# Banded attention: scores of even and odd heads issued alternately into two PSUM banks, softmax by token tile, and one pool of eight PSUM banks

## The chip, the cores and the metric

The kernel runs on one core of one Trainium2 chip. The metric is device time in microseconds (us), from the start of the program to its end; the median of the runs counts. The core has a matrix engine (TensorE, PE in the profile, with its weight loads as PEld), a vector engine (VectorE, DVE), an activation engine (ScalarE, ACT), a general one (GpSimd, POOL), and a queue engine that issues DMAs (SyncE, SP). Matmul results land in PSUM, which has eight banks of 128 x 512 float32.

## The reference, cut to what matters

One sequence of 512 tokens with 1024 channels passes two blocks of two layers each: a gated recurrence with a convolution, cross-attention to a memory, feed-forward layers, a second gated recurrence, and then, near the end, the layer of this change, a causal sliding-window attention with 16 query heads of 64 channels, two key/value heads, a window of 128, a bias by distance and a sink logit for each head. Cut:

```
q = (h @ w_q)                                   # 16 heads of 64, in two groups of 8
s = q k^T / 8  over 128 queries x 256 keys      # the block before and the block itself
s = where(mask, s + bias, NEG)
m = max(max(s), sink);  p = exp(s - m)
p = p / (sum(p) + exp(sink - m))
out = (p @ v) @ w_out
```

After it come a last layer of 1024 to 4096 to 1024 channels and a norm.

## The kernel before, in words

Everything is float32. A product is made of three matmuls (`mm3`, lines 180 to 182): each operand is split into a high part (`split`, L152, ScalarE) and the rest (L153, VectorE), and high x high, high x low and low x high are added up in PSUM. Weights come by DMA into `raw`, are split into `w` tiles (`chunk`) and used by `lin_a` (output channels on partitions, four banks at once), `lin_b` (tokens on partitions) or `lin_out` (the last product of a layer, with residual and norm). The order of the instructions on each engine is not written by hand: a scheduler runs through the program with its own estimate of times, takes what is ready by the order in the text (moved by `later` and by `ahead`), and gives a tile its place in a pool when its first writer is issued. Each engine then runs its own list in that order, with semaphores between.

PSUM is divided into two pools. `mm` has five banks (`bank`), for the projections and for the accumulators of attention and recurrence; `aux` has three (`xbank`), for transposes, scores and other short-lived results. SBUF has a pool `big` of 16 slots of 8 KB a partition, from which most activations come, the score tiles `s` among them.

The banded attention is `swa` (L931). Keys are computed once and laid out twice, on partitions 0 to 63 and 64 to 127, as `K`; values lie in `vz`. For each of the two groups of 8 heads (j = 0, 1) `q_proj(j)` makes the queries `qh`, `ql`, in which an even head has partitions 0 to 63 and its odd neighbour 64 to 127, and `attend(j)` calls `swa_heads` (L995). That goes through eight units (t, e): four tiles of 128 tokens, and for each the even (e = 0) and the odd (e = 1) four heads. `soft` makes the scores of a unit: twice a bank with two heads, six matmuls of 64 rows by 256 keys; VectorE scales the bank and adds the bias into `s` (L1014); then maximum (L1017, L1018), exponentials on ScalarE (L1021), sums and sink (L1023 to L1026), and the division, half on VectorE (L1029), half on ScalarE (L1031). `apply` transposes `s` (L1043), splits it into `pT` (tiles of `ring`, one for each e), and multiplies by the values into `po`, one bank for a whole token tile, which is split into `oh`, `ol` after e = 1. `staged` (its fourth argument is 2 here) writes `soft` of two units ahead of each `apply`. `q_proj(1)` stands behind `attend(0)` in the text, and `attend(1)` lies inside `lin_out` of the output projection, behind its early part, which multiplies the first half of the heads into four banks that stay open.

Of the kernel before, what the change touches and what calls it, by code (L numbers as in the profile page):

```python
# [10 lines left out]
F32 = mybir.dt.float32  # L11
# [3 lines left out]
ALU = mybir.AluOpType  # L15
# [57 lines left out]
class Net:  # L73
    def __init__(self, tc, a, ctx):
        self.tc, self.nc, self.a = tc, tc.nc, a
        pool = lambda name, bufs, **kw: ctx.enter_context(tc.tile_pool(name=name, bufs=bufs, **kw))
        self.const = pool("const", 1)
        self.wp = pool("wp", 4)
        self.rawp = pool("rawp", 3)
        self.big = pool("big", 16)  # L80
        self.work = pool("work", 2)
        self.small = pool("small", 4)
        self.mm = pool("mm", 5, space=bass.MemoryType.PSUM)
        self.aux = pool("aux", 3, space=bass.MemoryType.PSUM)
        self.n = 0
        nc = self.nc
        self.consts = self.const.tile([128, NCONST], F32, name="consts")
        nc.sync.dma_start(self.consts[:, :DEC], a["consts"][:, :DEC])
        self.ident = self.consts[:, IDENT:IDENT + 128]
        self.steps = self.const.tile([128, 256], F32R, name="steps")  # L90
        nc.scalar.activation(self.steps, self.consts[:, TRI:TRI + 256], AF.Copy)
        self.gains_T = self.const.tile([128, 40], F32, name="gains_T")
        self.half = self.const.tile([128, 8], F32, name="half")
        nc.gpsimd.memset(self.half, -0.5)
        self.r = []
        for t in range(4):
            self.r.append(self.const.tile([128, 1024], F32, name=f"r{t}"))
            nc.sync.dma_start(self.r[t], a["x"][0, t * 128:(t + 1) * 128, :])
            if t == 1:
                self.first = self.chunk(a["ab_w_in"][0], 2560, ahead=0)  # L100
# [29 lines left out]
        return bank  # L130

    def xbank(self, shape):
        return self.aux.tile(shape, F32, tag="aux", name=self.nm("aux"))

    def bload(self, dst, ap):
        self.nc.sync.dma_start(dst, ap.unsqueeze(0).broadcast_to(list(dst.shape)))
# [156 lines left out]
        else:  # L293
            self.nc.vector.tensor_tensor(r, r, ps, ALU.add)  # L294

# [1 line left out]

    def hgrn_mixer(self):
        nc, a = self.nc, self.a
# [504 lines left out]
            first = False  # L804


# [1 line left out]

    def gla_prepare(self):
        nc, a = self.nc, self.a  # L810
# [184 lines left out]
    def swa_heads(self, j, qh, ql, K, vz, bias, sink, nsink, oh, ol):  # L995
        nc = self.nc
        po = self.ready(self.bank([128, 4, 128]))

        def keys(t):
            k0 = max(t - 1, 0) * 128  # L1000
            return (k0, 0, 256) if t else (k0, 128, 128)

        def soft(u):
            t, e = u
            tk = slice(t * 128, t * 128 + 128)
            k0, off, n = keys(t)
            rows = slice(64 * e, 64 * e + 64)
            s = self.slot([128, 4, 256], name="s")
            for i in range(0, 4, 2):
                ps = self.xbank([128, 2, 256])  # L1010
                for d in range(2):
                    self.mm3(ps[:, d, :], qh[rows, i + d, tk], ql[rows, i + d, tk],
                             K[rows, j, 0, k0:k0 + 256], K[rows, j, 1, k0:k0 + 256], True, True)
                nc.vector.scalar_tensor_tensor(s[:, i:i + 2, :n], ps[:, :, :n], 0.125,  # L1014
                                               bias[:, e, i:i + 2, off:off + n], ALU.mult, ALU.add)
            mx = self.st([128, 4], "mx4")
            nc.vector.reduce_max(mx, s[:, :, :n], axis=AX.X)  # L1017
            nc.vector.scalar_tensor_tensor(mx, mx, -1.0, nsink[:, j, e], ALU.mult, ALU.min)  # L1018
            sm = self.st([128, 4], "sm4")
            for h in range(4):  # L1020
                nc.scalar.activation(s[:, h, :n], s[:, h, :n], AF.Exp, bias=mx[:, h:h + 1],  # L1021
                                     accum_out=sm[:, h:h + 1])
            nc.vector.tensor_tensor(mx, mx, sink[:, j, e], ALU.add)  # L1023
            nc.scalar.activation(mx, mx, AF.Exp)
            nc.vector.tensor_tensor(sm, sm, mx, ALU.add)
            nc.vector.reciprocal(sm, sm)  # L1026
            for h in range(4):
                if h < 2:
                    nc.vector.tensor_scalar(s[:, h, :n], s[:, h, :n], sm[:, h:h + 1], None, ALU.mult)  # L1029
                else:  # L1030
                    nc.scalar.activation(s[:, h, :n], s[:, h, :n], AF.Identity, scale=sm[:, h:h + 1])  # L1031
            return s

        def apply(u, s):
            t, e = u
            tk = slice(t * 128, t * 128 + 128)
            k0, off, n = keys(t)
            nk = n // 128
            p = self.ring[e]
            for kt in range(nk):  # L1040
                ps = self.xbank([128, 4, 128])
                for i in range(4):
                    nc.tensor.transpose(ps[:, i, :], s[:, i, kt * 128:kt * 128 + 128], self.ident)  # L1043
                self.split(p[:, 0, kt], p[:, 1, kt], ps)
            c = slice(64, 192) if e == 0 else slice(0, 128)
            for kt in range(nk):
                kb = k0 // 128 + kt
                self.mm3(po, vz[0][:, kb, j, c], vz[1][:, kb, j, c], p[:, 0, kt], p[:, 1, kt],
                         kt == 0 and e == 0, kt == nk - 1 and e == 1)
            if e == 1:  # L1050
                self.split(oh[:, :, tk], ol[:, :, tk], po)

        self.staged([(t, e) for t in range(4) for e in range(2)], soft, apply, 2)


def body(tc, a, out, stop=None):
# [66 lines left out]
```

## Time and profile before

| | |
|---|---|
| time, median of 3 runs | 2504.81 us (2504.08 to 2505.48) |
| span of the profiled execution, first to last instruction | 2503.4 us |
| mean granted TensorE clock | 0.993 |
| busy share: PE, PEld, DVE, ACT, POOL | 98%, 82%, 50%, 38%, 7% |
| DMA, mean over the span | 96 GB/s |

Times of instructions are counted from the start of the span, which is 1.4 us shorter than the median. Matmuls are pipelined: a row's duration reaches from its start to the landing of its results, so that a matmul of 0.28 us can be followed by the next after 0.12 us; what TensorE can do in a time is read from the distance of starts. A row "x2" merges neighbours of the same kind. In brackets stands how long the engine had waited for nothing but another engine, and which.

### The profile page before, as it was taken

What the parts mean: (1) busy time and instruction counts of PE and PEld (TensorE: products, weight loads), DVE (VectorE), ACT (ScalarE), POOL (GpSimd) and SP (SyncE); (2) the same over time, 40 slices, a digit from 0 to 9 for tenths busy, and PEclk for the clock granted to TensorE, in tenths of its full rate; (3) what the DMA queues carried; (4) which work ended last, traced back from release to release, by engine and by line L of the source; (5) the groups of instructions that cost most, each with busy time, mean ns of one, the idle gap of its engine ahead of it and who ended that gap; (6) DMA issues with size and microseconds to landing.
All of it is one profiled execution on the core that took longest, in us unless ns stands there. A gap on an engine that the chain in (4) does not pass through costs nothing.

```text
span 2503.4 us, 30298 instructions
## 1 busy us (share of the span) xinstructions
PE 2458.3 (98%) x12334; PEld 2052.4 (82%) x12334; DVE 1249.7 (50%) x1772; ACT 944.6 (38%) x1576; POOL 181.3 (7%) x219
## 2 busy tenths in 40 slices
PE   8989999999999999999999999999999999999998
PEld 8876787888888997888888786888888877888887
DVE  4798566433326766433327423444444467444443
ACT  3643343222223343322224634433223456423323
POOL 1151300000000100000001003100000100000000
PEclk9999899999999999999999999999999999999999
DMA  6323122333324332233223223233222421222222
GB/s 214 109 102 102 53 85 77 92 99 95 99 74 144 123 130 76 85 101 99 95 76 121 69 85 43 76 101 101 93 101 98 142 74 51 72 97 95 99 93 84
DMA packets 121788, 239.48 MB, mean 96 GB/s; under 512 B 7849, under 2 KB 14309, under 8 KB 121392
## 3 DMA queue, kind: packets, MB, share of 16 engines
q1 hardware_dynamic: 118976, 229.73, 28.3%
q0 software_dynamic: 2096, 6.76, 1.4%
q8 instruction: 97, 1.59, 0.3%
q10 hardware_dynamic: 576, 1.05, 0.1%
q14 instruction: 43, 0.35, 0.0%
HBM read 234.34 MB, written 6.32 MB: 96 GB/s over the span
## 4 chain that ended last, share of the span: by engine, by line
PE 90%; DVE 6%; issue 1%; ACT 1%; DMA 1%; POOL 0%; SPq 0%; POOLq 0%; DVEq 0%; ACTq 0%
PE mm L180 28%; PE mm L181 27%; PE mm L182 27%; DVE acc L525 2%; PE aux L254 2%; PE aux L581 1%; DVE w L153 1%; PE aux L180 1%; PE mm L608 1%; PE mm L605 1%; PE aux L182 1%; PE aux L181 1%; DVE bn L275 0%; PE aux L1043 0%; DMA raw<-in_ffn_wg 0%
## 5 line engine op out<-in xcount | busy, mean ns | idle before, releaser
L153 DVE TENSOR_TENSOR w<-raw,w 128x1024 fp32r<-128x1024 f32 (+1 forms) x286 | 341.0, 1195 | 604.4 <-ACT w L152 604.1
L181 PE MATMUL mm<-xTl,w 128*128 128x512 f32 (+1 forms) x1696 | 614.0, 363 | 2.2 <-DVE xTl L153 2.2
L180 PE MATMUL mm<-xTh,w 128*128 128x512 f32 (+1 forms) x1696 | 610.4, 363 | 1.0 <-ACT w L152 0.8
L182 PE MATMUL mm<-xTh,w 128*128 128x512 f32 (+1 forms) x1696 | 605.7, 362 | 0.0
L152 ACT ACTIVATE w<-raw 128x1024 fp32r<-128x1024 f32 (+1 forms) x286 | 293.8, 1029 | 748.8 <-PE mm L182 598.3
L181 PEld LDWEIGHTS mm<-xTl,w 128*128 128x128 f32 x1696 | 321.5, 190 | 50.8 <-DVE xTl L153 2.4
L180 PEld LDWEIGHTS mm<-xTh,w 128*128 128x128 f32 x1696 | 320.9, 190 | 50.4 <-ACT w L152 1.2
L182 PEld LDWEIGHTS mm<-xTh,w 128*128 128x128 f32 x1696 | 319.4, 189 | 48.8
L181 PE MATMUL mm<-w,hidh 128*128 128x512 f32 x752 | 292.0, 389 | 0.0
L180 PE MATMUL mm<-w,hidh 128*128 128x512 f32 x752 | 291.1, 389 | 0.0
L182 PE MATMUL mm<-w,hidl 128*128 128x512 f32 x752 | 288.9, 389 | 0.0
L173 DVE SCALAR_TENSOR_TENSOR w<-raw,gains_T,w 128x512 fp32r<-128x512 f32 (+1 forms) x200 | 139.0, 738 | 212.0 <-ACT w L172 211.3
L172 ACT ACTIVATE w<-raw,gains_T 128x512 fp32r<-128x512 f32 (+1 forms) x200 | 131.3, 707 | 237.3 <-PE mm L182 220.9
L182 PEld LDWEIGHTS mm<-w,hidl 128*128 128x128 f32 x752 | 141.2, 188 | 29.3
L180 PEld LDWEIGHTS mm<-w,hidh 128*128 128x128 f32 x752 | 141.2, 188 | 29.2
L181 PEld LDWEIGHTS mm<-w,hidh 128*128 128x128 f32 x752 | 141.2, 188 | 29.1
L180 PE MATMUL mm<-w,xTh 128*128 128x512 f32 (+1 forms) x352 | 135.1, 386 | 0.0
L181 PE MATMUL mm<-w,xTh 128*128 128x512 f32 (+1 forms) x352 | 135.1, 384 | 0.0
L182 PE MATMUL mm<-w,xTl 128*128 128x512 f32 (+1 forms) x352 | 134.8, 384 | 0.0
L294 DVE TENSOR_TENSOR r<-r,mm 128x512 f32<-128x512 f32 x112 | 76.3, 686 | 72.8 <-PE mm L182 72.7
L525 DVE SCALAR_TENSOR_TENSOR acc<-u,pack,acc 128x511 f32<-128x511 f32 (+29 forms) x90 | 83.7, 972 | 0.0
L180 PEld LDWEIGHTS mm<-w,xTh 128*128 128x128 f32 x352 | 66.5, 189 | 15.5 <-issue 2.3
(323 smaller groups left out, 3344.9 us busy)
## 6 DMA issues: line engine op xcount, KB each, us to landing
raw<-in_w_up SPq DMA_DIRECT2D x64, 512.0 KB, 3.6
raw<-in_w_down SPq DMA_DIRECT2D x64, 512.0 KB, 3.2
raw<-in_ffn_wd SPq DMA_DIRECT2D x44, 512.0 KB, 3.2
raw<-in_ffn_wg SPq DMA_DIRECT2D x40, 512.0 KB, 3.6
raw<-in_ffn_wu SPq DMA_DIRECT2D x40, 512.0 KB, 3.5
raw<-in_ab_w_in SPq DMA_DIRECT2D x24, 512.0 KB, 3.8
raw<-in_a_w_in SPq DMA_DIRECT2D x24, 512.0 KB, 3.6
raw<-in_xa_wk SPq DMA_DIRECT2D x16, 512.0 KB, 3.3
```

The lines of the kernel that those rows point to most:

```text
L152: self.nc.scalar.activation(hi, src, AF.Copy)
L153: self.nc.vector.tensor_tensor(lo, src, hi.bitcast(F32), ALU.subtract)
L172: nc.scalar.activation(u[:, 0, i], raw[:, i], AF.Identity, scale=g)
L173: nc.vector.scalar_tensor_tensor(u[:, 1, i], raw[:, i], g, u[:, 0, i].bitcast(F32), ALU.mult, ALU.subtract)
L180: nc.tensor.matmul(ps, lh, rh, start=start, stop=False)
L181: nc.tensor.matmul(ps, lh, rl, start=False, stop=False)
L182: nc.tensor.matmul(ps, ll, rh, start=False, stop=stop)
L254: self.nc.tensor.transpose(ps[:, j, :], src[:, j * 128:j * 128 + 128], self.ident)
L294: self.nc.vector.tensor_tensor(r, r, ps, ALU.add)
L525: nc.vector.scalar_tensor_tensor(dst, src, col, dst, ALU.mult, ALU.add)
L581: nc.tensor.matmul(d[:, h - h0, :], ke[rows, t, h * 128:h * 128 + 128], vh(t, h)[rows, :], start=True, stop=True)
L605: nc.tensor.matmul(o, P[:, h, :], vh(t, h), start=True, stop=False)
```

## The change

The two PSUM pools become one, `mm`, with eight banks; `xbank` takes its banks from it. In `swa_heads`, `soft` is cut in two. `scores(t)` makes the scores of all eight heads of a token tile, with two `s` tiles and, for each pair of heads, two banks, one for e = 0 and one for e = 1; the three products are issued alternately for e = 0 and e = 1. `soft(t, e, s)` is the rest of the softmax. `staged` now goes by token tile: `first(t)` makes both scores and both softmaxes, `second(t)` applies both, and one tile is written ahead (its default). The number of matmuls, evictions and softmax instructions is the same. Two headings in comments are taken out, so that lines shift.

```diff
--- before.py
+++ after.py
@@ -80,8 +80,7 @@
         self.big = pool("big", 16)
         self.work = pool("work", 2)
         self.small = pool("small", 4)
-        self.mm = pool("mm", 5, space=bass.MemoryType.PSUM)
-        self.aux = pool("aux", 3, space=bass.MemoryType.PSUM)
+        self.mm = pool("mm", 8, space=bass.MemoryType.PSUM)
         self.n = 0
         nc = self.nc
         self.consts = self.const.tile([128, NCONST], F32, name="consts")
@@ -130,7 +129,7 @@
         return bank
 
     def xbank(self, shape):
-        return self.aux.tile(shape, F32, tag="aux", name=self.nm("aux"))
+        return self.mm.tile(shape, F32, tag="mm", name=self.nm("aux"))
 
     def bload(self, dst, ap):
         self.nc.sync.dma_start(dst, ap.unsqueeze(0).broadcast_to(list(dst.shape)))
@@ -293,7 +292,7 @@
         else:
             self.nc.vector.tensor_tensor(r, r, ps, ALU.add)
 
-    # ---- block one -----------------------------------------------------------------
+
 
     def hgrn_mixer(self):
         nc, a = self.nc, self.a
@@ -804,7 +803,7 @@
             first = False
 
 
-    # ---- block two -----------------------------------------------------------------
+
 
     def gla_prepare(self):
         nc, a = self.nc, self.a
@@ -1000,19 +999,25 @@
             k0 = max(t - 1, 0) * 128
             return (k0, 0, 256) if t else (k0, 128, 128)
 
-        def soft(u):
-            t, e = u
+        def scores(t):
             tk = slice(t * 128, t * 128 + 128)
             k0, off, n = keys(t)
-            rows = slice(64 * e, 64 * e + 64)
-            s = self.slot([128, 4, 256], name="s")
+            both = [self.slot([128, 4, 256], name="s") for _ in range(2)]
             for i in range(0, 4, 2):
-                ps = self.xbank([128, 2, 256])
+                ps = [self.xbank([128, 2, 256]) for _ in range(2)]
                 for d in range(2):
-                    self.mm3(ps[:, d, :], qh[rows, i + d, tk], ql[rows, i + d, tk],
-                             K[rows, j, 0, k0:k0 + 256], K[rows, j, 1, k0:k0 + 256], True, True)
-                nc.vector.scalar_tensor_tensor(s[:, i:i + 2, :n], ps[:, :, :n], 0.125,
-                                               bias[:, e, i:i + 2, off:off + n], ALU.mult, ALU.add)
+                    for a, b, start, stop in ((qh, 0, True, False), (qh, 1, False, False), (ql, 0, False, True)):
+                        for e in range(2):
+                            rows = slice(64 * e, 64 * e + 64)
+                            nc.tensor.matmul(ps[e][:, d, :], a[rows, i + d, tk], K[rows, j, b, k0:k0 + 256],
+                                             start=start, stop=stop)
+                for e in range(2):
+                    nc.vector.scalar_tensor_tensor(both[e][:, i:i + 2, :n], ps[e][:, :, :n], 0.125,
+                                                   bias[:, e, i:i + 2, off:off + n], ALU.mult, ALU.add)
+            return both
+
+        def soft(t, e, s):
+            k0, off, n = keys(t)
             mx = self.st([128, 4], "mx4")
             nc.vector.reduce_max(mx, s[:, :, :n], axis=AX.X)
             nc.vector.scalar_tensor_tensor(mx, mx, -1.0, nsink[:, j, e], ALU.mult, ALU.min)
@@ -1029,7 +1034,6 @@
                     nc.vector.tensor_scalar(s[:, h, :n], s[:, h, :n], sm[:, h:h + 1], None, ALU.mult)
                 else:
                     nc.scalar.activation(s[:, h, :n], s[:, h, :n], AF.Identity, scale=sm[:, h:h + 1])
-            return s
 
         def apply(u, s):
             t, e = u
@@ -1050,7 +1054,17 @@
             if e == 1:
                 self.split(oh[:, :, tk], ol[:, :, tk], po)
 
-        self.staged([(t, e) for t in range(4) for e in range(2)], soft, apply, 2)
+        def first(t):
+            both = scores(t)
+            for e in range(2):
+                soft(t, e, both[e])
+            return both
+
+        def second(t, both):
+            for e in range(2):
+                apply((t, e), both[e])
+
+        self.staged(range(4), first, second)
 
 
 def body(tc, a, out, stop=None):
```

## Rows read from the trace of the kernel before

**Rows 1.** The page, engines: busy us, share of the span, instructions.
```profile
PE 2458.3 (98%) x12334; PEld 2052.4 (82%) x12334; DVE 1249.7 (50%) x1772; ACT 944.6 (38%) x1576; POOL 181.3 (7%) x219
```

**Rows 2.** The page, chain that ended last, shares by engine.
```profile
PE 90%; DVE 6%; issue 1%; ACT 1%; DMA 1%; POOL 0%; SPq 0%; POOLq 0%; DVEq 0%; ACTq 0%
```

**Rows 3.** Busy time by stretch: length, PE, PEld, DVE, ACT, POOL, clock, DMA.
```profile
2002.00:2057.00 55.00, 51.61 (x253) 39.79 (x251) 36.59 (x81) 31.89 (x93) 1.49 (x2) 0.94 0.26 86
2057.00:2131.00 74.00, 72.90 (x379) 56.94 (x378) 55.57 (x126) 49.34 (x144) 0.74 (x2) 1.00 0.14 45
```

**Rows 4.** Timeline of PE: start us, duration us, line, tiles, shape, count.
```profile
2012.16 0.28 PE L182 MATMUL aux<-K,ql 64*128 64x256 f32 x1
2012.37 0.49 PE L181 MATMUL mm<-xTl,w 128*128 128x512 f32 x1
2012.79 0.38 PE L180 MATMUL aux<-K,qh 64*128 64x256 f32 x1
2013.01 0.28 PE L181 MATMUL aux<-K,qh 64*128 64x256 f32 x1
2013.13 0.28 PE L182 MATMUL aux<-K,ql 64*128 64x256 f32 x1
```

**Rows 5.** Timeline of PE at 2006.4 to 2006.7 us.
```profile
2006.44 0.28 PE L182 MATMUL aux<-K,ql 64*128 64x256 f32 x1
2006.45 0.38 PE L181 MATMUL aux<-K,qh 64*128 64x256 f32 x2
2006.57 0.38 PE L182 MATMUL aux<-K,ql 64*128 64x256 f32 x2
2006.68 0.28 PE L180 MATMUL aux<-K,qh 64*128 64x256 f32 x1
```

**Rows 6.** Timeline of PE, first and last run of scores for j = 1.
```profile
2070.25 0.38 PE L180 MATMUL aux<-K,qh 64*128 64x256 f32 x1
...
2104.37 0.38 PE L180 MATMUL aux<-K,qh 64*128 64x256 f32 x1
```

**Rows 7.** Timeline of PE, the end of the attention for j = 0.
```profile
2035.62 0.39 PE L182 MATMUL mm<-xTh,w 128*128 128x512 f32 x1
...
2039.11 0.47 PE L180 MATMUL mm<-pT,vz 128*128 128x512 f32 x1 [1.98 <-DVE ol L153]
...
2055.38 0.51 PE L180 MATMUL mm<-pT,vz 128*128 128x512 f32 x1 [0.95 <-DVE ol L153]
...
2057.46 0.48 PE L180 MATMUL mm<-w,oh 128*128 128x512 f32 x1
```

**Rows 8.** Groups by line, 2002 to 2131, DVE: busy us, mean ns | idle before.
```profile
L1014 DVE SCALAR_TENSOR_TENSOR s<-aux,bias 128x512 f32<-128x512 f32 x24 | 16.3, 685 | 5.0 <-PE aux L182 4.8
L1017 DVE TENSOR_REDUCE mx<-s 128x4 f32<-128x1024 f32 x12 | 14.6, 1215 | 0.1
L1029 DVE TENSOR_SCALAR s<-s,sm 128x256 f32<-128x256 f32 x24 | 7.3, 349 | 0.1
```

**Rows 9.** Waits of PE over the span: us in total, times, longest.
```profile
PE aux L535 <- DVE pack L545: 3.4, 1, 3.4
PE mm L180 <- DVE qt L368: 3.1, 1, 3.1
...
PE aux L180 <- DVE pl L153: 2.0, 2, 1.0
```

**Rows 10.** Busy time by stretch, columns as in rows 3.
```profile
125.00:150.00 25.00, 18.39 (x96) 15.82 (x95) 25.00 (x32) 8.30 (x12) 11.57 (x7) 0.86 0.14 47
```

**Rows 11.** ACT: its timeline at 2053 us, and groups by line, 2002 to 2131.
```profile
2053.31 2.09 ACT L152 ACTIVATE qh<-mm 128x512 fp32r<-128x512 f32 x4
...
L1021 ACT ACTIVATE s<-s,mx 128x256 f32<-128x256 f32 x48 | 23.8, 502 | 3.5 <-DVE mx L1018 3.5
```

## The prediction

> **What bounds the kernel now.** I read the engine table of the page first: TensorE is busy for 98% of the span [rows 1], so a change pays where it takes work or waiting off TensorE, and elsewhere only if it ends a wait there. The chain that ended last says the same: 90% of it is TensorE [rows 2]. Then I cut the span into stretches. The two banded attentions (j = 0, then j = 1) lie at 2002 to 2131 us. In 2002 to 2057 TensorE is busy for 51.61 of 55 us at a mean granted clock of 0.94, in 2057 to 2131 for 72.90 of 74 at 1.00; VectorE is at about two thirds and three quarters [rows 3]. So the second attention is bound by TensorE's own work (other matmuls fill what its softmax leaves open), and the first has a stretch in which TensorE waits. Last I read TensorE's instructions one by one there.
>
> **The scores, one matmul.** One alone costs 0.12 us from start to start: 2013.01 to 2013.13 [rows 4]. There are 192 of them (two attentions, 4 token tiles, 8 heads, 3 products). Around them TensorE loses time at each change between these 64-row matmuls and 128-row ones. A lone 128-row matmul among scores shows it [rows 4]: the score before it lasts 0.21 instead of 0.12 (2012.16 to 2012.37), it lasts 0.42 instead of about 0.23 (to 2012.79), and the first score behind it 0.22 instead of 0.12 (to 2013.01). That is 0.09 + 0.19 + 0.10 = 0.38 us for each unbroken run of scores. I count 28 such runs in the trace, 14 in each attention.
>
> **The scores, two at a time.** The trace of before already holds what the change wants. For a moment at 2006.2 us the order of the instructions put scores of an even and an odd head side by side, and there two of them start 0.01 us apart: L182 at 2006.44 and L181 at 2006.45; the next pair follows about 0.12 later, the next again at 2006.68 [rows 5] (a merged row "x2" of 0.38 us holds two matmuls of 0.28, of which the second starts 0.10 to 0.11 after the first). So a pair takes 0.12 us, the time of one.
>
> **Change part 1, second attention (j = 1).** Its scores run from 2070.25 to 2105.27 in 14 runs, of which the first matmul of the first and of the last stand in the rows [rows 6]. Now: 96 x 0.12 + 14 x 0.38 = 16.8 us. Afterwards, all paired and each token tile in two runs: 48 x 0.12 + 8 x 0.38 = 8.8, a gain of 8.0. Low end: five banks stay held here (the accumulator `po` and the four of `lin_out`'s early part), as in the old pool of 5, so three of the eight are left; a first pair takes two, and of the second pair the even head finds a bank before the odd one does and may be issued alone. With half the pairs lost and 12 runs: 24 x 0.12 + 48 x 0.12 + 12 x 0.38 = 13.2, a gain of 3.6. I take 6.0, about the middle. It lies on the path, since TensorE is busy 72.90 of 74 us here [rows 3].
>
> **Change part 2, first attention (j = 0).** The same counting gives TensorE 4 to 8 us less work. But here the path is not TensorE alone. Its filler, the projection of the second query group, ends about 2035.6; then TensorE waits 1.98 and 0.95 us for the eviction of `po` (`ol`), which the change leaves as it is, and the next filler, the output projection, starts at 2057.46 [rows 7]. Saved score time ahead of 2036 only brings this stretch forward if its softmax comes forward too. I take 2.5. Upper end 7: 4 of TensorE plus most of the 55 - 51.61 = 3.4 us of idle time [rows 3], which output-projection matmuls could fill if the joint pool gives them a bank earlier. Lower end -10: the rival that ends slower, below.
>
> **Change part 3, softmax by token tile.** The count of VectorE and ScalarE instructions stays. The order moves: the four evictions L1014 of a token tile now come ahead of both maxima L1017, so head set 0 waits for two more evictions of 0.685 us, 1.37, before its maximum [rows 8]. Queued behind them on VectorE are that maximum and the weight splits, and ScalarE's exponentials wait for it. In the second attention TensorE has the output projection as cover, so I cost this at nothing there; without that cover it is 1.37 x 4 = 5.5 us an attention. No DMA is added or moved past another by hand; the order on every queue is the scheduler's.
>
> **Change part 4, one pool of eight banks.** It acts on the whole kernel, since the scheduler gives a freed bank to whichever tile is ready. Three waits of TensorE in before can only be waits for a bank, as the waiting matmul does not read what the releaser wrote: L535 for `pack` 3.4 us, L180 for `qt` L368 3.1, L180 for `pl` 2.0 [rows 9]. Upper end 8.5. But the first two lie where VectorE is busy for 25.00 of 25 us [rows 10], so what is late next is VectorE, and most comes back as another wait. Lower end -6.5: two waits of that size where a transpose finds every bank held by projections. I take 2.0.
>
> **Sum.** 6.0 + 2.5 + 0 + 2.0 = 10.5 us off the profiled span of 2503.4 us: 2492.9. The median of the runs is 2504.8, so 1.4 us lie around the span: 2494.3.
>
> **Rivals.**
> *Bound by the evictions.* A bank of scores takes VectorE 0.685 us [rows 8], two 1.37; paired scores fill two banks in 0.72, unpaired in 1.44. If nothing else is at hand for TensorE, the score stage then ends with VectorE and each of 16 groups gains 1.44 - 1.37 = 0.07: 1.1 us, hence 2503.7 us. For it speaks the wait at 2036 to 2057, against it that TensorE is nearly always busy otherwise [rows 3]. [...] The rows of the second attention, with filler to hand, speak against it there.
>
> *The alternation does not come out.* The scheduler orders by its own estimate of when a bank is free; if the odd head's bank always comes late, the matmuls run singly and only 12 of 28 runs are saved, 12 x 0.38 = 4.6 us of TensorE, half of it off the path: 2502.5. Against it: the pairs of rows 5 came out unasked.
>
> *Slower: room in the pool of 16 big slots.* In the first attention I count 14 held: four of `xT`, two `vz`, `K`, two of queries, two of the ring, `bias`, `oh`, `ol`. Two are left, exactly one token tile's pair of `s`. So the scores of the next tile, issued ahead, cannot be evicted before the present tile is transposed, and at three tile boundaries a whole unit's softmax is exposed: VectorE 2 x 0.685 + 1.215 + 2 x 0.349 = 3.3 [rows 8] and four exponentials of 0.50 on ScalarE [rows 11], 5.3 us each, 15.9 in all. Less the 6.0 of part 1 that is 9.9 slower: 2503.4 + 9.9 + 1.4 = 2514.7. It turns the sign once the three boundaries expose 8.0 together, 2.7 each. For it: the query eviction (four `qh`, L152) follows only at 2053.31 [rows 11], 17 us after its matmuls ended. Against it: before lives on two or three `s` tiles as well, and once the second projection is done four slots come free.
>
> **How the numbers follow.** About 0.2% (5.0 us) is what a measurement of this kernel can tell from no change. Forecast 0.60, with a range of its own of 2483 to 2499; eviction bound 0.17; no alternation 0.06; slower 0.15; the 0.02 left go to a small gain from the pool alone. So faster 0.62, same 0.23, slower 0.15. All upper ends together give 8.0 + 7 + 8.5 = 23.5 us: 2481.3. The range reaches from 2481 to 2511, which leaves out the outer part of the slow case.
>
> **What would show it.** Step 1: rows of 64x256 matmuls in pairs 0.01 us apart, and their total start-to-start time near 18 to 25 us where it is now near 34. Fewer runs of scores: 16 to 22 in place of 28. Step 2: TensorE's idle time in the first attention, and whether the output projection starts before the second query eviction. Step 4: the three bank waits gone, and whether VectorE stays at 25 of 25 us in 125 to 150. I am wrong if scores are paired and the attentions still end as late (eviction bound), if `s` tiles are waited for (slots), or if bank waits turn up in the projections, outside 2002 to 2131 us.

## The result, and the profile of the changed kernel

The changed kernel takes 2897.96 us (median of 4 runs, 2893.23 to 2900.9), the kernel before 2504.9. The ratio is 1.1568, 95% interval 1.1552 to 1.1584: 15.7% slower. The prediction was 2494.3 us, with a range of 2481 to 2511.

The profiled execution spans 2891.4 us, against 2503.4 before. The page of the changed kernel: engines (busy us, share of the span, instructions), the busy tenths of TensorE and its granted clock in 40 slices, and the shares of the chain that ended last.

```profile
PE 2585.9 (89%) x12334; PEld 2155.5 (75%) x12334; DVE 1267.9 (44%) x1772; ACT 952.3 (33%) x1576; POOL 188.8 (7%) x219
...
PE   8889779799997778799997799889999779799999
...
PEclk9997889899998789899998898989999889899999
...
PE 70%; DVE 4%; ACT 4%; POOL 2%; issue 1%; DMA 0%; POOLq 0%; ACTq 0%; DVEq 0%
```

The number of instructions on each engine is that of before [rows 1]. TensorE is busy 127.6 us longer with the same 12334 matmuls, and idle for 2891.4 - 2585.9 = 305.5 us instead of 2503.4 - 2458.3 = 45.1, 260.4 more. Together that is the 388.0 us by which the span grew. The holes lie in all parts of the program, in slices 5, 6, 13 to 17, 22 and 23 for example, and not only at the banded attention (slices 33 to 35). TensorE's share of the chain falls from 90% [rows 2] to 70%.

The waits of TensorE over the span of the changed kernel: line waited at, releaser, total us, times, longest.

```profile
PE aux L253 <- ACT z L478: 81.6, 16, 9.1
PE aux L253 <- DVE r L286: 77.1, 16, 9.7
PE aux L253 <- DVE tmp L693: 22.1, 11, 3.6
PE aux L1047 <- DVE s L1034: 18.2, 6, 7.2
PE aux L443 <- DVE r L286: 15.5, 3, 5.2
...
PE aux L440 <- DVE r L286: 6.0, 1, 6.0
```

L253 is the transpose in `transpose4` (L254 before). It waits for `r`, the residual after layer norm, or for `z`, the same after another norm: the last steps of a layer, in `lin_out` (the pooling layer writes them itself). With L443 and L440, the form that this step has ahead of the pooling layer, 81.6 + 77.1 + 15.5 + 6.0 = 180.2 us are waited for at layer ends. Before, the wait of a transpose for `r` came to 1.5 us in all. None of the waits shown is one for a bank: each matmul reads what its releaser wrote. The three bank waits of [rows 9] are gone from the list.

One layer end in both kernels shows what happened. First the changed kernel (timeline of TensorE; in brackets idle time before, and its releaser):

```profile
514.48 0.39 PE L180 MATMUL mm<-wb,oh 128*128 128x512 f32 x1
514.70 0.39 PE L181 MATMUL mm<-wb,ol 128*128 128x512 f32 x1
520.21 1.97 PE L253 MATMUL aux<-consts,r 128*128 128x128 f32 x8 [5.12 <-DVE r L286]
521.83 0.77 PE L179 MATMUL mm<-wb,oh 128*128 128x512 f32 x1
522.40 0.63 PE L180 MATMUL mm<-wb,oh 128*128 128x512 f32 x1
522.83 0.63 PE L181 MATMUL mm<-wb,ol 128*128 128x512 f32 x1
```

And VectorE of the changed kernel over the wait:

```profile
515.13 0.69 DVE L291 SCALAR_TENSOR_TENSOR r<-r,mm 128x512 f32<-128x512 f32 x1 [1.39 <-PE mm L181]
515.85 0.69 DVE L274 BATCH_NORM_STATS2 bn<-r 128x6 f32<-128x512 f32 x1
516.58 0.21 DVE L276 BATCH_NORM_AGGREGATE mv<-bn 128x2 f32<-128x12 f32 x1
516.82 1.28 DVE L285 SCALAR_TENSOR_TENSOR r<-r,mv,w4k 128x1024 f32<-128x1024 f32 x1
518.87 1.28 DVE L286 SCALAR_TENSOR_TENSOR r<-r,rs,w4k 128x1024 f32<-128x1024 f32 x1 [0.76 <-POOL rs L268]
```

The last matmul of one token tile's product starts at 514.70, its layer norm takes until 518.87 + 1.28 = 520.15, and the transposes of the result stand next in TensorE's list. The product of the next token tile (L179, `oh`), whose operands were all written before 496 us, stands behind them and starts at 521.83. The same layer end in the kernel before:

```profile
435.80 0.40 PE L181 MATMUL mm<-wb,oh 128*128 128x512 f32 x1
436.03 1.04 PE L254 MATMUL aux<-consts,r 128*128 128x128 f32 x8
436.83 0.47 PE L182 MATMUL mm<-wb,ol 128*128 128x512 f32 x1
```

There the transposes stand in the middle of the next product; when TensorE comes to them, `r` is ready, and nothing is waited for. Busy time around this layer end, columns as in [rows 3], first of before, then of the changed kernel:

```profile
428.00:488.00 60.00, 59.69 (x370) 53.49 (x369) 30.57 (x38) 16.38 (x25) 5.18 (x8) 1.00 0.26 79
```

```profile
500.00:560.00 60.00, 43.49 (x215) 37.24 (x215) 28.98 (x38) 8.07 (x11) 7.21 (x8) 0.83 0.16 51
```

In 60 us around the same layer end, before does 370 matmuls and the changed kernel 215.

The lists of instructions of the two programs say the same without times. 747 tiles are laid in PSUM, 462 by `bank` and 285 by `xbank`. Within one kind, the first writes of the tiles stand in TensorE's list in the order of the text, without an exception, in both kernels. Across the kinds, 243 tiles of the kernel before (227 of them from `xbank`) are first written behind a tile that the text makes later; with one pool there is 1. So with the joint pool products no longer pass transposes.

### The profile page after: what moved, and what is told of

It reads as the page before. It is cut to its first block, busy times and chain, and to the rows that moved or that the text cites. A ratio compares the mean times of both kernels' runs of the same rounds, so it can differ in the third digit from the quotient of the medians.

```text
span 2891.4 us, 30275 instructions
## 1 busy us (share of the span) xinstructions
PE 2585.9 (89%) x12334; PEld 2155.5 (75%) x12334; DVE 1267.9 (44%) x1772; ACT 952.3 (33%) x1576; POOL 188.8 (7%) x219
## 4 chain that ended last, share of the span: by engine, by line
PE 70%; DVE 4%; ACT 4%; POOL 2%; issue 1%; DMA 0%; POOLq 0%; ACTq 0%; DVEq 0%
PE mm L179 22%; PE mm L180 22%; PE mm L181 21%; PE aux L253 2%; DVE r L286 1%; POOL rs L265 1%; ACT s L1026 1%; ACT z L478 1%; POOL rs L268 1%; ACT z L453 1%; DVE r L293 1%; DVE bn L274 1%; PE aux L443 1%; PE aux L580 0%; DVE s L1015 0%
## 5 line engine op out<-in xcount | busy, mean ns | idle before, releaser
L179 PE MATMUL mm<-xTh,w 128*128 128x512 f32 (+1 forms) x1696 | 617.5, 364 | 0.0
L181 PE MATMUL mm<-xTh,w 128*128 128x512 f32 (+1 forms) x1696 | 615.3, 363 | 0.4 <-DVE w L152 0.4
L181 PEld LDWEIGHTS mm<-xTh,w 128*128 128x128 f32 x1696 | 323.4, 191 | 49.7 <-DVE w L152 0.6
L179 PEld LDWEIGHTS mm<-xTh,w 128*128 128x128 f32 x1696 | 323.8, 191 | 48.4
L179 PE MATMUL mm<-w,hidh 128*128 128x512 f32 x752 | 294.3, 392 | 0.0
L179 PEld LDWEIGHTS mm<-w,hidh 128*128 128x128 f32 x752 | 142.6, 190 | 29.6
L179 PE MATMUL mm<-w,xTh 128*128 128x512 f32 (+1 forms) x352 | 138.5, 394 | 0.0
L253 PE MATMUL aux<-consts,r 128*128 128x128 f32 x160 | 36.0, 401 | 84.0 <-DVE r L286 77.1
L253 PE MATMUL aux<-consts,z 128*128 128x128 f32 x128 | 30.1, 413 | 81.6 <-ACT z L478 81.6
```

The source lines that it names most:

```text
L179: nc.tensor.matmul(ps, lh, rh, start=start, stop=False)
L181: nc.tensor.matmul(ps, ll, rh, start=False, stop=stop)
L253: self.nc.tensor.transpose(ps[:, j, :], src[:, j * 128:j * 128 + 128], self.ident)
```

## Experiments

**Which half of the change it is.** Theory A: the joint pool makes the loss, by the order of first writes. Theory B: the new scores and the softmax by token tile make it. `e1_scores_only` has the new `swa_heads` and the old pools:

```diff
-        self.mm = pool("mm", 8, space=bass.MemoryType.PSUM)
+        self.mm = pool("mm", 5, space=bass.MemoryType.PSUM)
+        self.aux = pool("aux", 3, space=bass.MemoryType.PSUM)
...
-        return self.mm.tile(shape, F32, tag="mm", name=self.nm("aux"))
+        return self.aux.tile(shape, F32, tag="aux", name=self.nm("aux"))
```

> The changed kernel with the two PSUM pools of before put back (5 banks for projections, 3 for scores and transposes); scores alternate and the softmax goes by token tile, as in the change. Theory A (one pool hands its banks out in the order of the text, so that on TensorE a transpose whose input is late stands ahead of the next product): all of the loss comes from the pool, so this is 2485 to 2510 us. Rival B (the loss comes from softmax by token tile, exposed in the attention and passed on): near 2880 us. Rival C (each does a part): in between, 2600 to 2800.

`e2_pool_only` is the kernel before with these lines the other way round: one pool of eight and the old scores.

> The kernel before with one PSUM pool of eight banks; scores and softmax as before. Theory A: 2880 to 2920 us, as the changed kernel. Rival B: near 2505. Rival C: in between.

Measured: e1 2510.7 us, just above the range given for it, ratio 1.0007 (0.9995 to 1.0019); e2 2892.47 us, ratio 1.1548 (1.153 to 1.1566). To within the noise, all of the loss is the pool's. The waits of TensorE in e2 are those of the changed kernel:

```profile
PE aux L253 <- ACT z L478: 77.4, 15, 8.9
PE aux L253 <- DVE r L286: 77.1, 16, 9.7
```

**Number of banks, or order.** `e3_five_two` is the kernel before with a bank less for transposes and scores. If the loss came from banks that are short for them, it should go the same way.

```diff
-        self.aux = pool("aux", 3, space=bass.MemoryType.PSUM)
+        self.aux = pool("aux", 2, space=bass.MemoryType.PSUM)
```

> The kernel before with two pools of 5 and 2 banks, one bank fewer for scores and transposes. Rival D (the joint pool is slow because projections take the banks that transposes need, so it is a matter of how many banks are left for them): a clear loss, 2560 us or more. Theory A (order, not number): two pools keep their separate orders and TensorE loses little: 2505 to 2530.

Measured: 2571.99 us, ratio 1.0274 (1.026 to 1.0288). That is outside the range of theory A and inside that of rival D: one bank less costs 2571.99 - 2505.75 = 66 us. Its waits are of another kind, many and small:

```profile
PE aux L254 <- DVE pack L545: 7.6, 1, 7.6
...
PE aux L254 <- DVE xTl L153: 4.5, 4, 3.0
```

So the number of banks matters, and more than was thought. This run alone does not rule rival D out for the joint pool; against it speak that the joint pool has no bank less than before, that its waits are for `r` and `z`, and the next two experiments.

`e8_two_tags` separates the pool from the kind of tile. It is the kernel before with one pool, in which the tiles of `xbank` keep a kind (a tag) and three banks of their own:

```diff
-        self.aux = pool("aux", 3, space=bass.MemoryType.PSUM)
...
-        return self.aux.tile(shape, F32, tag="aux", name=self.nm("aux"))
+        return self.mm.tile(shape, F32, tag="aux", name=self.nm("aux"), bufs=3)
```

> The kernel before with one PSUM pool that holds two kinds of tiles, five banks of the one and three of the other. Theory A (the order of the text holds within a kind of tile, not within a pool): as before, 2503 to 2507. If it held within the pool: near 2890.

Measured: 2505.51 us, ratio 0.9999 (0.999 to 1.0008). The order binds within a kind of tile, not within a pool. TensorE's list in e8 is that of before, matmul by matmul. (The kind gives the transposes an order of their own and three banks of their own at once; which of the two it is, the next experiment tells.)

**Is it the place in the text?** If the joint pool makes the order of the text TensorE's order, the loss must shrink when the text puts the transposes later. `e4_turn_later` is the changed kernel, in which `lin_out` keeps the transposes of a finished token tile back for two products:

```diff
+        rest = []
...
-                ev(t, p)
+                rest.append((n + 2, ev(t, p)))
+            while rest and rest[0][0] <= n:
+                turn = rest.pop(0)[1]
+                if turn:
+                    turn()
+        for _, turn in rest:
+            if turn:
+                turn()
```

(`ev` and the functions `nxt` now return the transposes as a function instead of making them.)

> The changed kernel, its one pool of eight banks kept; only the text of the last product of a layer is changed: the transposes of a token tile stand two products later in it (for tiles 0 and 1 behind the products (0,2) and (0,3), for tile 2 behind the last product, tile 3 as before). Theory A: the waits of about 5 us (8 to 9 where the input is z) ahead of the transposes of tiles 0 to 2 go, some 24 of 32, with the slow clock behind each; about 100 us of idle time and 40 of slow clock come back: 2740 to 2790 us. The waits in the pooling layer, whose text stays, stay. Rival D (too few banks for the transposes): no bank is added, so 2880 to 2920.

Measured: 2708.23 us, ratio 1.0811 (1.0796 to 1.0826), 190 us less than the changed kernel and more of a gain than expected. The waits of e4 (all lines lie some 8 to 16 lower):

```profile
PE aux L261 <- DVE r L294: 41.2, 8, 9.7
PE aux L261 <- ACT z L491: 20.9, 8, 4.3
PE aux L261 <- DVE tmp L709: 20.6, 11, 3.6
```

`r` and `z` fall from 158.7 to 62.1 us, with no bank added. What `lin_out` does not write stays as it was: `tmp` of the cross-attention 22.1 and now 20.6, and, of the 41.2 for `r`, the four waits at the end of the pooling layer, whose place the edit keeps: 25.2 us in both kernels. About half of the loss, 2708.23 - 2505.75 = 202 us, is still there in e4, with these waits and with others on data.

`e13_later_two_pools` is the control: the same later place in the kernel before, with its two pools.

> The control for e4_turn_later: the kernel before, two pools of 5 and 3 banks and its own scores, with the transposes of a token tile two products later in the text of a layer's last product, as there. Theory A: with pools of their own the transposes stand in nobody's way and their place in the text decides little: 2500 to 2515 us. If the later place is a gain in itself, as it was worth 190 us with the joint pool: clearly under 2490.

Measured: 2508.11 us, ratio 1.0008 (0.9997 to 1.0018). Where the scheduler may let products pass, the place in the text is worth nothing that can be measured; the 190 us are an effect of the joint pool.

**The clock.** After the wait of 5.12 us above, the matmuls start 0.43 us apart (522.40, 522.83), and 0.227 us apart in before. Two stretches of the changed kernel, ahead of and behind that wait (columns as in [rows 3]):

```profile
505.00:520.00 15.00, 9.03 (x43) 6.96 (x42) 12.52 (x16) 3.21 (x4) 3.61 (x4) 0.93 0.24 71
```

```profile
520.00:526.00 6.00, 5.79 (x20) 4.99 (x21) 1.54 (x3) 1.20 (x2) 0.00 (x0) 0.60 0.00 0
```

The granted clock is 0.60 in the second: 0.50 up to 524.8 us and 1.00 from there. Over the span TensorE stands at half clock for 450.4 us, and for 38.6 before (sum of the trace's clock records). `e10_warm` is the changed kernel with 36 more matmuls of 128 x 256, written into the bank of the transposes ahead of the first of a layer end, where TensorE waits for nothing. The order of the other matmuls in TensorE's list is the same but for 63 places, and the transposes overwrite the results.

```diff
-    def transpose4(self, src):
+    def transpose4(self, src, warm=0):
         ps = self.xbank([128, 4, 128])
+        for _ in range(warm):
+            self.nc.tensor.matmul(ps[:, 0:2, :], self.steps[:, 0:128], self.steps, start=True, stop=True)
```

> The changed kernel with one pool of eight banks, and 36 additional matmuls of 128x256 into the bank of the transposes, ahead of the first transposes of each token tile at the end of a layer (not in the pooling layer); they read what is long there, so that TensorE works through most of the 5 us in which it waited. Theory K (part of the loss is the clock that falls to half in such a wait and stays there for some 4 us behind it): the waits of the kernel stay in length, the clock behind them is full, some 24 waits give back about 2 us each: 2840 to 2865 us. If the clock plays no part: 2890 to 2910.

Measured: 2851.84 us, ratio 1.1378 (1.1362 to 1.1395): 46 us less with 1152 matmuls more (13486 against 12334). The waits at these places shrink, the extra work standing in them, and the one at the pooling layer, which has none, stays:

```profile
PE aux L255 <- ACT z L480: 17.0, 4, 4.7
PE aux L255 <- DVE r L288: 16.9, 13, 5.6
PE aux L445 <- DVE r L288: 15.5, 3, 5.2
```

So keeping TensorE busy in these waits is worth some 46 us of the loss, by the clock: its mean is 0.951 in e10 and 0.922 in the changed kernel. Half clock still holds for 279.6 us in e10; how much of the 127.6 us of longer busy time is the clock's was not taken apart by a run. From the traces: 336.7 us of TensorE's busy time lie at half clock in the changed kernel, 33.0 in before; half of the 303.7 more is 151.9, and by the starts, 0.43 us apart instead of 0.227, 143 of it are lost, so the clock is enough for all of the 127.6.

**What the scores would have brought.** The rest is about the part on which the prediction spent most, with the old pools, where it can be seen. `e7_not_alternated` is e1 with the scores of even heads first and those of odd heads behind: softmax and scores by token tile, without the alternation.

```diff
-                for d in range(2):
-                    for a, b, start, stop in ((qh, 0, True, False), (qh, 1, False, False), (ql, 0, False, True)):
-                        for e in range(2):
-                            rows = slice(64 * e, 64 * e + 64)
-                            nc.tensor.matmul(ps[e][:, d, :], a[rows, i + d, tk], K[rows, j, b, k0:k0 + 256],
-                                             start=start, stop=stop)
+                for e in range(2):
+                    rows = slice(64 * e, 64 * e + 64)
+                    for d in range(2):
+                        self.mm3(ps[e][:, d, :], qh[rows, i + d, tk], ql[rows, i + d, tk],
+                                 K[rows, j, 0, k0:k0 + 256], K[rows, j, 1, k0:k0 + 256], True, True)
```

> As e1_scores_only, but the scores of the even heads are issued before those of the odd ones: the softmax by token tile alone. The 24 pairs of e1_scores_only are worth at most 24 x 0.12 = 2.9 us. If softmax by token tile costs nothing: 2505 to 2508. If it costs what the pairs of e1_scores_only bring: 2510 to 2515.

`e5_tied` makes sure of the alternation. A product of one column claims each of the two banks, and the twelve matmuls are held behind the second claim, so that they can start only when both banks are there (the first score overwrites the claimed column):

```diff
+                for e in range(2):
+                    rows = slice(64 * e, 64 * e + 64)
+                    claim = nc.tensor.matmul(ps[e][:, 0, :1], self.ident[rows, :], self.ident[rows, :1],
+                                             start=True, stop=True)
+                with self.tc.issue_after(getattr(claim, "ins", claim)):
...
```

> Two PSUM pools of 5 and 3 banks as in e1_scores_only, and the pair of banks is claimed first: two matmuls of one column take both banks, and the scores of the pair are queued behind them, so that none starts until both are to be had. In e1_scores_only 24 of 96 pairs start together. Theory P (the scores' time on TensorE is on the path, and three banks kept the pairs apart): all 96 pairs, the scores' start-to-start time falls from 29 to about 17 to 19 us, and of these 10 us most come back: 2494 to 2503 us. Rival Q (the attention is bound by evictions and softmax, and by waits on TensorE that slow its clock): the pairs come, the time stays at 2505 to 2513.

`e6_tied_units` is e5 with the softmax by unit, as in before (`staged` over (t, e) with 2, the scores made at e = 0):

```diff
-        self.staged(range(4), first, second)
+        self.staged([(t, e) for t in range(4) for e in range(2)], first, apply, 2)
```

> As e5_tied, but the softmax goes by unit again: softmax and application of even and odd heads stand in the text as in the kernel before (two units ahead), only the scores of a token tile are made together. Theory R (softmax by token tile leaves TensorE waiting at the boundaries): 3 to 8 us less than e5_tied. Otherwise the same within 2 us.

`e9_first_pair` does without the claims: the first score of each bank is itself the claim, and the other ten are held behind that pair.

```diff
+                with self.tc.issue_after(pair(*todo[0])):
+                    for w in todo[1:]:
+                        pair(*w)
```

> As e5_tied (pools of 5 and 3 banks, pairs of banks tied), but without its 32 claiming matmuls: the first score of the even and of the odd head claim the two banks, and the other ten are queued behind the second of them. In e5_tied the scores' time fell by 12.9 us, and from the first score to the first matmul of the last layer by 1.8 only. If the claims cost the larger part of the difference: 2 to 4 us less than e5_tied, 2500 to 2503 us. If waits and the slow clock behind them take it: as e5_tied, 2503 to 2507.

`e12_first_pair_units` is e9 with the softmax by unit.

> As e9_first_pair, but softmax and application by unit as in the kernel before. e6_tied_units was 1 us above e5_tied, inside its interval: the same is expected here, within 2 us of e9_first_pair. If softmax by token tile costs TensorE waits that pairs do not repay: 2 to 5 us less.

Measured, with three counts from the traces: the 192 score matmuls' distance from start to start, summed; how many pairs start less than 0.03 us apart; and the stretch from the first score to the first matmul of the last layer of 1024 to 4096 channels.

| kernel | time us | ratio (interval) | scores us | pairs | stretch us |
|---|---|---|---|---|---|
| before | 2504.9 | | 30.5 | 4 | 143.6 |
| e8_two_tags (list of before) | 2505.51 | 0.9999 (0.999 to 1.0008) | 30.3 | 4 | 145.0 |
| changed | 2897.96 | 1.1568 (1.1552 to 1.1584) | 30.9 | 53 | 192.9 |
| e7_not_alternated | 2509.28 | 1.0015 (1.0004 to 1.0026) | 29.5 | 24 | 150.1 |
| e1_scores_only | 2510.7 | 1.0007 (0.9995 to 1.0019) | 29.3 | 24 | 147.9 |
| e5_tied | 2505.16 | 0.9999 (0.999 to 1.0007) | 17.6 | 69 | 141.8 |
| e6_tied_units | 2506.14 | 1.0006 (0.9997 to 1.0015) | 17.6 | 69 | 143.4 |
| e9_first_pair | 2501.7 | 0.9985 (0.9975 to 0.9994) | 22.8 | 86 | 138.8 |
| e12_first_pair_units | 2501.05 | 0.9984 (0.9973 to 0.9994) | 23.1 | 86 | 140.7 |

(Each ratio is to before on the same chip. Counts and stretch are those of one profiled execution of each. The sums of the scores hold waits between them: 0.2 us in before, 3.0 in e9 and e12, none in e5. In e7, as in before, the pairs come of the scheduler's own order. In e5 and e6 the twelve scores of all groups stand in pairs in TensorE's list; 69 start that close.) One stretch of the second attention in e9 shows the pairs at work, TensorE's timeline:

```profile
2066.13 0.39 PE L182 MATMUL mm<-w,ol 128*128 128x512 f32 x1
2066.45 0.50 PE L1012 MATMUL aux<-K,qh 64*128 64x256 f32 x3
2066.67 0.39 PE L1012 MATMUL aux<-K,ql 64*128 64x256 f32 x2
2066.79 0.51 PE L1012 MATMUL aux<-K,qh 64*128 64x256 f32 x4
2067.03 0.39 PE L1012 MATMUL aux<-K,ql 64*128 64x256 f32 x2
2067.15 0.28 PE L1012 MATMUL aux<-K,qh 64*128 64x256 f32 x1
2067.35 0.50 PE L181 MATMUL mm<-pT,vz 128*128 128x512 f32 x1
```

Twelve scores take 0.90 us from 2066.45 to 2067.35, switch at the end included. And the same stretch as in [rows 3], whole, first of before, then of e1 and of e9 (its two parts):

```profile
2002.00:2131.00 129.00, 124.51 (x629) 96.73 (x628) 92.15 (x205) 81.23 (x235) 2.23 (x4) 0.97 0.19 62
```

```profile
2002.00:2131.00 129.00, 123.95 (x603) 94.63 (x602) 91.58 (x202) 80.23 (x233) 2.23 (x4) 0.91 0.19 63
```

```profile
2002.00:2057.00 55.00, 50.21 (x272) 37.76 (x270) 38.88 (x90) 35.26 (x107) 1.49 (x2) 0.97 0.24 77
2057.00:2131.00 74.00, 68.54 (x370) 51.49 (x371) 52.73 (x116) 48.50 (x133) 1.48 (x4) 0.98 0.15 43
```

e1 gets 603 matmuls done where before does 629, at a granted clock of 0.91 against 0.97; e9 does 642, at 0.97 and 0.98 (its first score comes 1.3 us earlier than that of before).

What follows is limited by the noise of single executions: e8 has the list of before on TensorE, and its stretch is 1.4 us longer. Also, the stretches of e1, e7, e9 and e12 hold 16 transposes of the next layer's `z` where that of before holds 24; the other eight stand behind the end, some 0.8 us.

The stretch of e7 is 150.1 - 143.6 = 6.5 us longer than that of before; over all runs e7 is slower by 0.04 to 0.26%, 1.0 to 6.5 us. In the stretch TensorE's idle time rises from 4.5 to 7.2 us and its time at half clock from 6.8 to 23.9 (10.2 in e8); half of the 17.1 more, 8.6 us, is what that loses at most where TensorE always has work. So the clock is enough to account for most of the 6.5; it was not taken apart by a run of its own. Nor is it shown which part of e7 costs this, the softmax by token tile or the scores of a token tile made together, two banks at a time: once the pairs are sure, softmax by the unit has the longer stretch, by 1.6 and 1.9 us, which is little more than the noise (e6 against e5, e12 against e9).

The alternation as the change writes it gives 2.2 us of the stretch back (e1), little more than the noise; two full sets of banks for each group, 6.1 more (e5), and 9.1 without the claims (e9). In time, e5 came out as its rival Q has it, at 2505.16 and not at 2494 to 2503; e9, at 2501.7, agrees with the claims as the larger part of the difference. e9 and e12 lie 0.15% below before, with intervals that end just short of none; that is less than the 0.2% which the prediction takes as what can be told from no change.

## Why the prediction was wrong, point by point

**Part 4, one pool of eight banks: this step failed.** It was costed at 2.0 us gained, with ends of 8.5 gained and 6.5 lost; by e2 it costs 2892.47 - 2505.75 = 387 us (e2's time less that of before on the same chip). The step says that "the scheduler gives a freed bank to whichever tile is ready". The runs show that within one kind of tile the banks are given in the order of the text (none of 747 first writes out of order within a kind), so a joint kind puts all of TensorE's first writes into that order. I counted banks, where the kinds of tiles were what counted: two pools were also two orders that could pass each other, 243 times here. The lower end, "two waits of that size where a transpose finds every bank held by projections", had the wrong wait too: the transposes do not wait for a bank, and the products wait behind a transpose whose data is not there. The evidence was at hand. A row of before shows the transposes of one layer end in the middle of the next product (436.03, above), ahead of which the text has them; asking how they could come there could have led to it. The size comes mostly from there: 16 waits each for `r` and `z`, of 4.8 and 5.1 us on average, 158.7 us, with those ahead of the pooling layer 180.2 of the 260.4 us of added idle time, and the clock behind them, of which e10 gives back 46 us.

In the timeline above, nothing of the ready product starts in the 5.12 us of the wait.

**Bank waits in the projections, or not.** The list of signs names waits that turn up "in the projections, outside 2002 to 2131 us" as what would make the prediction wrong. Place and cause differ: it was the layer ends of the whole kernel, and no bank was waited for. The three bank waits of [rows 9] did go, and they are lost in the 388 us. VectorE has its stretch of full work later, and as full as in [rows 10]; this is the changed kernel:

```profile
150.00:180.00 30.00, 22.54 (x153) 21.93 (x152) 30.00 (x33) 11.78 (x17) 12.81 (x8) 0.83 0.32 107
```

**Parts 1 and 2, the scores in pairs: mechanism right, size off.** Pairs do start about 0.01 us apart as in [rows 5], and in the changed kernel 53 of 96 do (0.000 to 0.014 us), in 14 runs where I forecast 16 to 22. With the old pools and the change's text (e1), which is the case without the pool's loss, only 24 of 96 do, in 28 runs, as many as before, and no more than e7 has without any alternation in its text; I had taken half of them as the low end. Once both banks are tied together (e5, e9) they come: what kept them apart was that one side could start without the other. That comes near the rival "the alternation does not come out" (2502.5 us, with 12 of 28 runs saved; in e1 none is, and its ratio of 1.0007 has 1 in its interval). The summed distance of the scores in the changed kernel stays at 30.9 us, where 18 to 25 were forecast. But 8.3 us of it are waits, 7.2 of them behind the last score of one run, where transposes wait for `s`:

```profile
2345.20 0.28 PE L1012 MATMUL aux<-K,ql 64*128 64x256 f32 x1
2352.68 0.66 PE L1047 MATMUL aux<-consts,s 128*128 128x128 f32 x2 [7.20 <-DVE s L1034]
```

Without them it is 22.6 us, inside the forecast, at a granted clock of 0.83 from 2341 to 2421 us. (By this count before stands at 30.5 us, not "near 34" as the prediction has it.) Where the granted clock is 1.00 (2421 to 2422.64 us), a run of six pairs and six single scores reads:

```profile
2421.02 0.50 PE L1012 MATMUL aux<-K,qh 64*128 64x256 f32 x4
2421.36 0.28 PE L1012 MATMUL aux<-K,ql 64*128 64x256 f32 x2
...
2422.64 0.50 PE L180 MATMUL mm<-w,oh 128*128 128x512 f32 x1
```

18 scores in 1.62 us, 0.090 each instead of 0.12. When the pairs are made sure of (e9), the scores take 22.8 us, within the 18 to 25, and the stretch is 4.8 us shorter; 6.0 + 2.5 = 8.5 were forecast for both attentions. Without the waits between them the scores fall from 30.3 to 19.8 us, by 10.5; TensorE's idle time in the stretch rises from 4.5 to 10.2 us, by 5.7; 10.5 - 5.7 = 4.8. That this meets the 4.8 so exactly is luck, since 0.8 us of it are the transposes that lie behind the stretch in e9; over all runs e9 gains 0.15%, some 3.8 us.

With three banks to draw from, 24 of 96 pairs come in e1; with the same three and the pairs tied, 86 in e9.

**Part 3, softmax by token tile: taken at nothing, and perhaps too low.** With 5.5 us an attention as the price without cover, it was costed at nothing; the stretch of e7 is 6.5 us longer for both, and e7 as a whole 1.0 to 6.5 us slower. The cover was there (idle time rises by 2.7 us only), but time at half clock rises with it, from 6.8 to 23.9 us, which I had not counted. How much of this is the softmax's and how much that of the scores made together stays open.

**The rivals.** *Bound by the evictions* holds in a small part. Where the pairs come, a few waits for an evicted bank appear, 3.0 us in e9 (L1012 writes scores, L1022 is their eviction), about half of the 5.7 us by which idle time grew; this is e9 from 1995 to 2140 us:

```profile
PE aux L1012 <- DVE s L1022: 3.0, 2, 2.4
PE mm L181 <- DVE pT L153: 1.7, 3, 0.8
```

By that rival the scores would gain 1.1 us in all; e9 gains some 3.8 over all runs.

*Room in the pool of 16 slots* does not hold: it forecast 15.9 us of softmax that stands open at tile boundaries, which would show as transposes of `s` that wait. In e1, with the staging and the slots of the change, they wait 2.4 us in the whole stretch:

```profile
PE aux L1048 <- DVE s L1035: 1.9, 2, 1.2
PE aux L1048 <- ACT s L1037: 0.5, 1, 0.5
```

The 18.2 us for `s` at L1047 in the changed kernel look like that rival, but e1 shows that they come with the joint pool, not with the staging or the slots.

## What to carry to other kernels

Before two pools or kinds of tile are made one, ask not only how many places are free but what order the places are given in: a ready product can stand behind a transpose whose data comes 5 us later, as here, where TensorE started nothing else in a wait of 5.12 us. Look in the trace of before for work that stands ahead of what the text has earlier; each such place is one that the joint order takes away. A pair of matmuls that is to run together is best tied, so that neither starts until both have their bank: with three banks to draw from, 24 of 96 pairs came untied, 69 and 86 tied.

## What the runs showed of the hardware

Behind a wait of 5.12 us in the changed kernel TensorE's matmuls of 512 columns start 0.43 us apart instead of 0.227. The granted clock is 0.50 there, from 518.0 us, inside the wait, to 524.8, 4.6 us after TensorE's work sets in again, and 1.00 behind that; the starts from 524.89 us on are 0.23 apart. Half clock also came without long holes: in e7 and e1 idle time was only 2.7 and 0.6 us more than in before, in stretches of some 150, and time at half clock 17.1 us more in both. Part of that is chance: e8, with the list of before, has 3.4 us more of it than before.

A bank of PSUM less for transposes and scores (e3) makes the span 67.0 us longer on a kernel whose TensorE is busy for 98% of the time: 22.5 us of it idle time (2570.4 - 2502.8 = 67.6 against 45.1) and 44.5 longer busy time of the same matmuls, at a granted clock of 0.977 instead of 0.993.
